# One ring of eight PSUM banks for all stages of a macaron block, in place of one pool per stage

## The chip, the cores and the metric

The kernel runs on one core of one Trainium2 chip. The metric is the device time of one execution in microseconds; the time of the kernel before is the median of three runs, 1818.98 us (1816.17 to 1822.03).

## The reference

Sequence 1024, width 1024, one layer, everything in fp32. The layer is two gated feed-forward blocks with a mixer between them:

```python
h = x
h = h + 0.5 * swiglu_ffn(rmsnorm(h, ffn1_norm), ffn1_w_in, ffn1_w_out)      # d_ff = 2816
u = rmsnorm(h, mix_norm) @ w_mix_in                                         # 1024 x 3592
cb, cc, ch, gq, gk, gv, gz, gb, ga = split(u)
y_conv = rmsnorm_groups(cb * causal_conv3(cc * ch))                         # 512 channels
q, k, v = silu(causal_conv4([gq, gk, gv]))                                  # 4 heads of 128
y_gdn = rmsnorm(gated_delta_rule(l2norm(q), l2norm(k), v, g, beta)) * silu(gz)
h = h + concat([y_conv, y_gdn]) @ w_mix_out
h = h + 0.5 * swiglu_ffn(rmsnorm(h, ffn2_norm), ffn2_w_in, ffn2_w_out)
return rmsnorm(h, final_norm)
```

The gated delta rule is computed by chunks of the sequence: per chunk a masked, decayed product of the keys (`lower`), a triangular system with it, and a step of a state of 128 x 128 per head that goes from chunk to chunk. The kernel uses eight chunks of 128 positions.

## The kernel before

Each large fp32 product is made from three matmuls: an operand is split into a part `hi` and a rest `lo` (ScalarE makes `hi`, VectorE the difference), and `mm3` issues hi by hi, lo by hi and hi by lo, each 128 x 128 by 512 columns, into one PSUM bank (L197, L198, L199). The two feed-forward blocks and the q, k, v projection multiply 2 x 2 blocks by a scheme with seven products in place of eight; the sums of blocks that it needs are made on VectorE and GpSimd and partly kept in HBM.

There are three stages, each inside its own `with ExitStack()`, and each opens its own SBUF pool and its own PSUM pool through `scoped`:

- `f1`: the first feed-forward block (`ffn_in`, `ffn_out`), then the q, k, v projection and the gates (`project_ba`, `finish_ba`). All its banks come from one ring of eight, tag `ps`.
- `mx`: the mixer. Its pool has two rings: four banks `mm` and four banks `aux`. In `mm` lie the projections for z and the short convolution (`unit_steps`: one bank for 8 `mm3`, 24 matmuls), the small reductions of `conv_norm`, the output projection (`mix_out`: one bank for 4 `mm3`), and the column factors of the first half's norm (`norms2[0] = Norm(h2[0], "mm")`, `spread` at L269, read by eight VectorE instructions L305). In `aux` lie the products and transposes of the delta rule: seven tiles per chunk in `build` (decays L1117 and L1120, flips L1060, products L1054), five in `finish` (the blocks of the triangular inverse, L1080, L1261, L1269), five in `scan` (L1054, L1311, and one flip).
- `f2`: the second feed-forward block, again one ring of eight `ps`. The norm of the second half of its input (`norms2[1]`) is reduced and spread in this stage's first steps.

`mx` and `f2` begin with a VectorE memset of one column of their pool's first bank (L1015 and L1613).

The order of work in `mx` is written by hand as Python generators. `build(c)` for eight chunks runs in a pipeline with lag 3; at each step `pump` issues 2.2 `mm3` of the projections, and a step of `late_convs` (four-tap convolutions of v, k, q: ScalarE L953, three VectorE L955, ScalarE L957, store) is taken. Then comes one inversion of all 32 x 32 diagonal blocks on VectorE (`solve`), then `finish` and `scan` for eight chunks in a pipeline with lag 6, beside the remaining projections and `mix_out`. What is traced in this order is then ordered per engine by the framework's planner, ahead of time: it takes, on each engine, the earliest traced instruction that it reckons to be ready, and a tile is given a buffer of its ring only when it reckons one to be free. `tc.keep_in_program_order` holds an instruction behind all that was traced ahead of it on its engine; the reductions and the spreads of norms, the loads of weights (`load`) and the ScalarE part of each split carry it. On the chip each engine then follows its list, and waits by semaphores. A pool whose memory is that of an earlier pool can be used when the earlier pool's tiles have been released.

Of the kernel before, what the change touches and what calls it, by code (L numbers as in the profile page):

```python
# [7 lines left out]
F32 = mybir.dt.float32  # L8
# [4 lines left out]
P = 128  # L13
# [45 lines left out]
def tile_hybrid(  # L59
# [18 lines left out]
    nc = tc.nc  # L78
    PS = bass.MemoryType.PSUM
# [31 lines left out]
    def pool_tt(out, in0, in1, op):  # L111
        tc.keep_in_program_order(nc.gpsimd.tensor_tensor(out=out, in0=in0, in1=in1, op=op))  # L112
# [11 lines left out]
    def run_tasks(to=None, between=None):  # L124
        to = len(tasks) if to is None else to
        while done_to[2] < to:
            stage = 2
            if done_to[1] < min(done_to[2] + AHEAD_PREP + 1, len(tasks)):
                stage = 0 if done_to[0] < min(done_to[1] + AHEAD_LOAD - AHEAD_PREP + 1, len(tasks)) else 1
            f = tasks[done_to[stage]][stage]  # L130
            done_to[stage] += 1
            if f is not None:
                f()
            if stage < 2:
                continue
            if between is not None:
                between()


    scope = {}  # L140

    def psum(tag="ps"):
        bufs = {"ps": 8, "mm": 4, "aux": 4}[tag]
        return scope["ps"].tile([P, 512], F32, name=f"ps_{tag}", tag=tag, bufs=bufs)

    def temp4(dt, name):
        return scope["temp"](dt, name)
# [1 line left out]
    def temp(dt, name):  # L149
        return temp4(dt, name)[:, 3:HALF + 3]  # L150
# [20 lines left out]
    def vcol(i):  # L171
        return vs[:, i:i + 1]
# [16 lines left out]
    def tick():  # L189
        count[0] += 1  # L190
        due = [f for n, f in queue if n <= count[0]]
        queue[:] = [e for e in queue if e[0] > count[0]]
        for f in due:
            f()
# [14 lines left out]
    class Norm:  # L209
# [17 lines left out]
        def reduce(self):  # L227
            cp = psum(self.bank)
            for b in range(4):
                tc.keep_in_program_order(  # L230
                    nc.tensor.matmul(out=cp[:, b:b + 1], lhsT=self.acc[:, b * P:(b + 1) * P], rhs=ones[:, 0:1],
                                     start=True, stop=True))
            self.factor(cp[:, 0:4])
# [9 lines left out]
        def all_landed(self):  # L243
            cp = psum(self.bank)
            for b in range(4):
                tc.keep_in_program_order(
                    nc.tensor.matmul(out=cp[:, b:b + 1], lhsT=self.acc[:, b * P:(b + 1) * P], rhs=one,
                                     start=True, stop=True))
            self.factor(cp[:, 0:4])
# [14 lines left out]
        def spread(self, pinned=True):  # L264

            self.rb = psum(self.bank)
            for b in range(4):
                tc.keep_in_program_order(
                    nc.tensor.transpose(out=self.rb[:, b * P:(b + 1) * P],  # L269
                                        in_=self.rs[:, b:b + 1].broadcast_to([P, P]), identity=ident))  # L270
            for f in self.waiting:
                f()
# [18 lines left out]
    class Blocks:  # L291
# [8 lines left out]
        def gain(self, d):  # L300
            return vcol(self.g + d)
# [398 lines left out]

    def scoped(stack, name, temps=0):
        scope["sb"] = stack.enter_context(tc.tile_pool(name=name, bufs=1))
        scope["ps"] = stack.enter_context(tc.tile_pool(name=name + "ps", bufs=1, space=PS))
        scope["temp"] = lambda dt, n: scope["sb"].tile([P, HALF + 4], dt, name=n, tag="t", bufs=temps)

    def residual(src):

        tiles = [[None] * KT for _ in range(NH)]

        def fill(hf, d):  # L710
            tiles[hf][d] = slot(F32, "h")
            nc.sync.dma_start(out=tiles[hf][d], in_=src[hf][d])

        return tiles, fill
# [4 lines left out]
    h_dr = [[dram.tile([P, HALF], F32, name=f"h_dr{hf}{d}") for d in range(KT)] for hf in range(NH)]  # L719
    with ExitStack() as stack:  # L720
        scoped(stack, "f1", TEMPS)
        x = Blocks(h, "ffn1")
        norms = [Norm(h[hf]) for hf in range(NH)]
# [288 lines left out]

    with ExitStack() as stack:
        scoped(stack, "mx")
        nc.vector.memset(psum("mm")[:, 0:1], 0.0)  # L1015
        mx = scope["sb"]

        def halo(dt, name):
# [591 lines left out]

    with ExitStack() as stack:
        scoped(stack, "f2", TEMPS)
        nc.vector.memset(psum()[:, 0:1], 0.0)  # L1613
        acc, fill = residual(h2_dr)
        last = [Norm(acc[hf]) for hf in range(NH)]

        def pre_scaled(d):
            return d % 3 == 1

        def gain(hf, d):  # L1620
            a = acc[hf][d]
            nc.scalar.activation(out=a, in_=a, func=AF.Copy, scale=vcol(V_N["final"] + d))

        def scale_out(hf, cut=slice(0, HALF)):
            rb = temp(F32, "rbs")
            nc.scalar.copy(out=rb[:, cut], in_=last[hf].rb[:, cut])
            for d in range(KT):
                a = acc[hf][d][:, cut]
                if pre_scaled(d):
                    nc.gpsimd.tensor_tensor(out=a, in0=a, in1=rb[:, cut], op=ALU.mult)  # L1630
                else:
                    nc.vector.scalar_tensor_tensor(out=a, in0=a, scalar=vcol(V_N["final"] + d),
                                                   in1=last[hf].rb[:, cut], op0=ALU.mult, op1=ALU.mult)
                nc.sync.dma_start(out=out[hf, d][:, cut], in_=a)

        def out_t1():
            for d in range(KT):
                last[0].square(d)
            last[0].after(14, 4)
            last[0].then(lambda: [gain(0, d) for d in range(KT) if pre_scaled(d)] and scale_out(0))  # L1640

        def out_t2(d):
            if d == KH - 1:
                last[1].held = temp(F32, "sq")
                nc.scalar.activation(out=last[1].held, in_=acc[1][d], func=AF.Square)
            else:
                last[1].square(d, nc.vector)
            if pre_scaled(d):
                gain(1, d)

        ffn_out(acc, fill, g_dr, w2_out, out_t1, out_t2, by_tile=True)
        run_tasks()

        sums = [psum() for _ in range(2)]
        rbs = [psum() for _ in range(2)]
        ends = [temp(F32, "rbs") for _ in range(2)]
        for n, src in enumerate((last[1].acc, last[1].held)):
            for b in range(4):
                nc.tensor.matmul(out=sums[b // 2][:, b % 2:b % 2 + 1], lhsT=src[:, b * P:(b + 1) * P],
                                 rhs=ones[:, 0:1], start=(n == 0 and b % 2 == 0), stop=(n == 1),  # L1660
                                 skip_group_check=True)
        for i in range(2):
            ms, rs = (const.tile([P, 2], F32, name=f"{n}{i}") for n in ("last_ms", "last_rs"))
            nc.vector.tensor_scalar(out=ms, in0=sums[i][:, 0:2], scalar1=1.0 / D, scalar2=EPS,
                                    op0=ALU.mult, op1=ALU.add)
            nc.gpsimd.tensor_tensor(out=rs, in0=ms, in1=pneg[:, 0:2], op=ALU.pow)
            for b in range(2):
                nc.tensor.transpose(out=rbs[i][:, b * P:(b + 1) * P], in_=rs[:, b:b + 1].broadcast_to([P, P]),
                                    identity=ident)
            nc.scalar.copy(out=ends[i][:, 0:2 * P], in_=rbs[i][:, 0:2 * P])  # L1670
        for i in range(2):
            two = slice(2 * i * P, (2 * i + 2) * P)
            for d in (0, 1, 2, 3, 4, 5, 6, 7):
                a = acc[1][d][:, two]
                if pre_scaled(d):
                    pool_tt(a, a, ends[i][:, 0:2 * P], ALU.mult)
                else:
                    nc.vector.scalar_tensor_tensor(out=a, in0=a, scalar=vcol(V_N["final"] + d),
                                                   in1=rbs[i][:, 0:2 * P], op0=ALU.mult, op1=ALU.mult)
                if i:  # L1680
                    (nc.scalar if d in (1, 2, 5, 7) else nc.sync).dma_start(out=out[1, d], in_=acc[1][d])
        while queue:
            tick()
# [65 lines left out]
```

## Time and profile before

| what | value |
|---|---|
| median of three runs | 1818.98 us (1816.17 to 1822.03) |
| profiled execution | 1819.9 us, span 1818.2 us |
| granted TensorE clock, mean | 0.996 |
| PE busy | 1786.2 us (98%) |
| PE weight loads busy | 1456.0 us (80%) |
| DVE busy | 1333.0 us (73%) |
| ACT busy | 736.7 us (41%) |
| POOL busy | 540.0 us (30%) |
| HBM | 174 GB/s over the span |

The span runs from the first to the last instruction of the program; some 1.7 us of the execution lie around it. Matmuls overlap in the trace: one of 512 columns takes 0.39 us from start to end, but the next one starts 0.23 us after it, so a busy PE need not be at its peak, while a gap of PE is time in which nothing ran. `mx` goes from about 780 to 1168 us of the span.

### The profile page before, as it was taken

To read this page: it belongs to the slowest core of one execution; us is meant where nothing else is said; L and a number is where in the kernel's file an instruction comes from. 1 tells how busy PE (TensorE), PEld (TensorE's weight loads), DVE (VectorE), ACT (ScalarE), POOL (GpSimd) and SP (SyncE) were. 2 spreads that over 40 slices of the span, in tenths; PEclk is the share of its full clock that TensorE was granted. 3 is DMA by queue.
4 is the path that set the end of the run, shared out by engine and by line. 5 is a ranking of instruction groups with operands and counts; after the bars stand their busy time and mean duration, and the time that the engine had idled before them with its cause. 6 is when DMAs were issued, how large, how long until landed. Compare 5 with 4: busy or idle time off the path is not lost.

```text
span 1818.2 us, 24794 instructions
## 1 busy us (share of the span) xinstructions
PE 1786.2 (98%) x8476; PEld 1456.0 (80%) x8476; DVE 1333.0 (73%) x2090; ACT 736.7 (41%) x1471; POOL 540.0 (30%) x382
## 2 busy tenths in 40 slices
PE   9999999999999999999999999999999999999997
PEld 6887788888888877777888877788888888888886
DVE  7898877678776889889575556797666666677675
ACT  7532322223534554468424433552222232344443
POOL 0000034446331412302211102016445554435252
PEclk9999999999999999999999999999999999999998
DMA  7445544336984543478753675523433444487642
GB/s 277 163 129 174 179 146 134 127 116 217 329 270 133 163 156 100 150 239 275 240 186 101 215 255 179 165 73 128 159 125 116 144 140 133 165 304 272 203 143 89
DMA packets 198255, 318.74 MB, mean 175 GB/s; under 512 B 28528, under 2 KB 49008, under 8 KB 198128
## 3 DMA queue, kind: packets, MB, share of 16 engines
q1 hardware_dynamic: 195104, 311.85, 52.0%
q10 hardware_dynamic: 3024, 5.30, 0.8%
q8 instruction: 67, 1.10, 0.3%
q14 instruction: 60, 0.49, 0.1%
HBM read 230.54 MB, written 86.53 MB: 174 GB/s over the span
## 4 chain that ended last, share of the span: by engine, by line
PE 86%; DVE 4%; DMA 4%; ACT 3%; issue 1%; SPq 1%; POOL 1%; POOLq 0%; ACTq 0%; DVEq 0%
PE ps_ps L197 24%; PE ps_ps L199 24%; PE ps_ps L198 24%; PE ps_mm L197 3%; PE ps_mm L198 3%; PE ps_mm L199 3%; DMA raw<-w_in 2%; PE ps_aux L1054 1%; DVE wlo L105 1%; DMA qkv_dr<-cv 1%; PE ps_aux L1060 1%; DVE T L117 1%; DMA gd<-qkv_dr 1%; DVE cv L955 1%; PE ps_aux L1080 0%
## 5 line engine op out<-in xcount | busy, mean ns | idle before, releaser
L197 PE MATMUL ps_ps<-hi,whi 128*128 128x512 f32 x1400 | 547.8, 392 | 5.4 <-DVE c L467 2.8
L199 PE MATMUL ps_ps<-hi,wlo 128*128 128x512 f32 x1400 | 544.7, 390 | 1.0 <-DVE wlo L105 1.0
L198 PE MATMUL ps_ps<-lo,whi 128*128 128x512 f32 x1400 | 545.2, 389 | 0.1
L197 PEld LDWEIGHTS ps_ps<-hi,whi 128*128 128x128 f32 x1400 | 262.8, 188 | 67.7 <-DVE c L467 6.2
L199 PEld LDWEIGHTS ps_ps<-hi,wlo 128*128 128x128 f32 x1400 | 262.8, 188 | 59.2 <-DVE wlo L105 4.5
L198 PEld LDWEIGHTS ps_ps<-lo,whi 128*128 128x128 f32 x1400 | 262.8, 188 | 54.8 <-DVE lo L733 0.6
L112 POOL TENSOR_TENSOR T<-raw 128x512 f32<-128x512 f32 x112 | 173.1, 1546 | 447.2 <-DMA raw<-w_in 225.4
L105 DVE TENSOR_TENSOR wlo<-raw,whi 128x512 fp32r<-128x512 f32 x280 | 238.7, 862 | 71.0 <-ACT whi L104 69.6
L105 DVE TENSOR_TENSOR wlo<-T,whi 128x512 fp32r<-128x512 f32 x244 | 212.6, 883 | 87.2 <-ACT whi L104 85.6
L199 PE MATMUL ps_ps<-ghi,wlo 128*128 128x512 f32 x616 | 241.2, 392 | 0.8 <-DVE wlo L105 0.8
L197 PE MATMUL ps_ps<-ghi,whi 128*128 128x512 f32 x616 | 241.2, 391 | 0.0
L198 PE MATMUL ps_ps<-glo,whi 128*128 128x512 f32 x616 | 240.6, 391 | 0.0
L104 ACT CAST whi<-T 128x512 fp32r<-128x512 f32 x244 | 146.5, 616 | 125.2 <-PE ps_ps L198 41.8
L104 ACT CAST whi<-raw 128x512 fp32r<-128x512 f32 x280 | 168.7, 617 | 58.6 <-PE ps_ps L198 14.6
L105 DVE TENSOR_TENSOR glo<-raw,ghi 128x512 fp32r<-128x512 f32 x154 | 127.7, 829 | 47.2 <-ACT ghi L104 46.6
L197 PE MATMUL ps_mm<-hi,whi 128*128 128x512 f32 x384 | 157.8, 411 | 2.2 <-DVE u L478 1.2
L198 PE MATMUL ps_mm<-lo,whi 128*128 128x512 f32 x384 | 151.9, 396 | 0.0
L199 PE MATMUL ps_mm<-hi,wlo 128*128 128x512 f32 x384 | 151.7, 395 | 0.0
L199 PEld LDWEIGHTS ps_ps<-ghi,wlo 128*128 128x128 f32 x616 | 115.8, 188 | 27.4 <-DVE wlo L105 2.0
L198 PEld LDWEIGHTS ps_ps<-glo,whi 128*128 128x128 f32 x616 | 115.9, 188 | 25.6
L197 PEld LDWEIGHTS ps_ps<-ghi,whi 128*128 128x128 f32 x616 | 115.8, 188 | 25.2
L104 ACT CAST ghi<-raw 128x512 fp32r<-128x512 f32 x154 | 95.0, 617 | 71.1 <-DMA raw<-f1A 19.0
(256 smaller groups left out, 2116.9 us busy)
## 6 DMA issues: line engine op xcount, KB each, us to landing
raw<-w_in SPq DMA_DIRECT2D x264, 256.0 KB, 4.3
raw<-w_out SPq DMA_DIRECT2D x154, 256.0 KB, 4.2
raw<-w_qkv SPq DMA_DIRECT2D x36, 256.0 KB, 3.4
f1S<-S SPq DMA_DIRECT2D x33, 256.0 KB, 4.1
raw<-f1A SPq DMA_DIRECT2D x33, 256.0 KB, 3.8
raw<-f1S SPq DMA_DIRECT2D x33, 256.0 KB, 3.5
f2S<-S SPq DMA_DIRECT2D x33, 256.0 KB, 4.8
raw<-f2A SPq DMA_DIRECT2D x33, 256.0 KB, 4.4
```

What stands on the lines that cost most here:

```text
L104: tc.keep_in_program_order(nc.scalar.copy(out=hi, in_=src))
L105: nc.vector.tensor_tensor(out=lo, in0=src, in1=hi.bitcast(F32), op=ALU.subtract)
L112: tc.keep_in_program_order(nc.gpsimd.tensor_tensor(out=out, in0=in0, in1=in1, op=op))
L117: nc.vector.tensor_tensor(out=out, in0=in0, in1=in1, op=op)
L197: nc.tensor.matmul(out=ps, lhsT=whi, rhs=xhi, start=start, stop=False, skip_group_check=True)
L198: nc.tensor.matmul(out=ps, lhsT=whi, rhs=xlo, start=False, stop=False, skip_group_check=True)
L199: nc.tensor.matmul(out=ps, lhsT=wlo, rhs=xhi, start=False, stop=stop, skip_group_check=True)
L955: nc.vector.scalar_tensor_tensor(out=acc, in0=u[:, i:i + HALF], scalar=vcol(wc + i), in1=acc, op0=ALU.mult, op1=ALU.add)
L1054: nc.tensor.matmul(out=ps[:, sl], lhsT=lhs[:, sl], rhs=rhs[:, sl], start=start, stop=stop)
L1060: nc.tensor.transpose(out=ps[:, sl], in_=src[:, sl], identity=ident)
```

## The change

The PSUM pools of the stages are replaced by one pool `banks`, opened once, with one ring of eight banks under one tag. The argument of `psum` no longer chooses a ring; it only enters the tile's name. `scoped` opens no PSUM pool any more, and the two memsets at the start of `mx` and `f2` are gone. All calls of `psum("mm")`, `psum("aux")` and `psum()` stay as they are, and so does the order in which work is traced. The SBUF pools are not touched.

```diff
+    banks = ctx.enter_context(tc.tile_pool(name="banks", bufs=1, space=PS))
+
-    def psum(tag="ps"):
-        bufs = {"ps": 8, "mm": 4, "aux": 4}[tag]
-        return scope["ps"].tile([P, 512], F32, name=f"ps_{tag}", tag=tag, bufs=bufs)
+    def psum(name="ps"):
+        return banks.tile([P, 512], F32, name=f"ps_{name}", tag="ps", bufs=8)
...
     def scoped(stack, name, temps=0):
         scope["sb"] = stack.enter_context(tc.tile_pool(name=name, bufs=1))
-        scope["ps"] = stack.enter_context(tc.tile_pool(name=name + "ps", bufs=1, space=PS))
...
         scoped(stack, "mx")
-        nc.vector.memset(psum("mm")[:, 0:1], 0.0)
...
         scoped(stack, "f2", TEMPS)
-        nc.vector.memset(psum()[:, 0:1], 0.0)
```

## The prediction

> **What bounds the kernel now.** I read the page's first part, then the list of PE's waits, the table of stretches, and the order of instructions around each wait that the change can touch.
>
> ```profile
> span 1818.2 us, 24794 instructions
> PE 1786.2 (98%) x8476; PEld 1456.0 (80%) x8476; DVE 1333.0 (73%) x2090; ACT 736.7 (41%) x1471; POOL 540.0 (30%) x382
> ```
>
> PE is busy for 1786.2 of 1818.2 us. The change removes no matmul, so it can win at most the 32.0 us in which PE stands still, and anything it costs must appear as new idle time of PE. The profiled execution took 1819.9 us, 1.7 us outside its span and 0.9 us above the median of the runs, 1818.98. I make the sum as a difference and give it for both.
>
> The longest waits of PE, and the shorter ones that concern banks, are these (microseconds in all, times, longest):
>
> ```profile
> PE ps_ps L197 <- DVE c L467: 2.8, 4, 1.6
> PE ps_ps L269 <- POOL rs L225: 1.8, 2, 1.2
> ...
> PE ps_aux L1060 <- DMA gd<-qkv_dr: 1.7, 3, 0.8
> PE ps_aux L1261 <- DVE x L1253: 1.7, 1, 1.7
> PE ps_ps L197 <- DVE h L1562: 1.5, 1, 1.5
> ...
> PE ps_mm L197 <- DVE u L478: 1.2, 1, 1.2
> PE ps_aux L1117 <- DVE r L1110: 1.1, 1, 1.1
> PE ps_aux L1054 <- DVE gd L1286: 1.1, 1, 1.1
> PE ps_mm L197 <- DVE h L305: 1.0, 1, 1.0
> PE ps_aux L1060 <- ACT gd L1333: 1.0, 1, 1.0
> ...
> PE ps_aux L1054 <- ACT junk L1146: 0.4, 1, 0.4
> ```
>
> Which of them are waits for a bank is seen from the code. The matmul of L197 into the first `mm` tile reads nothing that L478 makes; L478 is the last reader of an `f1` bank, so PE waits for the old pool to be given up. In the same way L1562 is the last reader of an `mx` bank ahead of `f2`. L305 reads the spread factors, a bank of the `mm` ring, and the matmuls of `mix_out` behind it read nothing of its result. L1146 reads a flip in `aux` that L1054 doesn't need. That makes four bank waits, 1.2 + 1.5 + 1.0 + 0.4 = 4.1 us. All the others are waits for data: L1253, L1286, L1110 and L1333 make what the waiting matmul reads, and no number of banks shortens them.
>
> Two stretches of the mixer, its build and its scans (columns: length, busy time and count of PE, PEld, DVE, ACT and POOL, granted clock, DMA share, GB/s):
>
> ```profile
> 800.00:860.00 60.00, 57.23 (x302) 46.18 (x303) 55.80 (x123) 52.88 (x128) 11.78 (x8) 1.00 0.86 274
> ...
> 1060.00:1130.00 70.00, 65.97 (x457) 53.28 (x453) 42.75 (x84) 27.79 (x77) 13.43 (x12) 0.98 0.65 205
> ```
>
> In the first, DVE (55.80 of 60) and ACT (52.88) are as full as PE (57.23): there a bank that comes free sooner still waits for its reader. In the second no engine but PE is near full, and PE loses 70.00 - 65.97 = 4.0 us to chains of dependent steps.
>
> **The change part by part.** *From `f1` to `mx`.*
>
> ```profile
> 779.75 0.39 PE L198 MATMUL ps_ps<-lo,whi 128*128 128x512 f32 x1
> 779.98 0.39 PE L199 MATMUL ps_ps<-hi,wlo 128*128 128x512 f32 x1
> 781.55 0.47 PE L197 MATMUL ps_mm<-hi,whi 128*128 128x512 f32 x1 [1.18 <-DVE u L478]
> ...
> 782.07 0.06 DVE L1015 MEMSET ps_mm<- 128x1 f32 x1
> ...
> 798.86 0.39 PE L198 MATMUL ps_mm<-lo,whi 128*128 128x512 f32 x1
> 800.36 0.50 PE L1117 MATMUL ps_aux<-r,mask 128*128 128x512 f32 x1 [1.11 <-DVE r L1110]
> ```
>
> The two PE starts are 1.57 us apart, where the first two rows show matmuls of this kind 0.23 us apart, so the pool's hand-over costs 1.34 us. With one ring the first `mm` tile takes any bank already evacuated. Does the gain survive the next wait, at 800.36 us, where PE stands until DVE has made r0? The rows show PE leaving a triple unfinished (L198 at 798.86, its L199 not yet issued) for L1117: the planner puts in `mm3` work until it reckons r0 ready. If PE comes free 1.34 us sooner in its reckoning too, it fits in some 1.34 / 0.23 = 6 more matmuls ahead of L1117, and these are then missing from later work. I take -1.3; the ends are 0 (L1117 keeps its place behind the same matmuls, and the wait of 1.11 grows) and -1.3.
>
> *The first half's norm in `mx`.*
>
> ```profile
> 1130.98 5.35 DVE L305 SCALAR_TENSOR_TENSOR h<-h,vs,ps_mm 128x512 f32<-128x512 f32 x8
> ...
> 1135.07 0.39 PE L199 MATMUL ps_mm<-hi,wlo 128*128 128x512 f32 x1
> ...
> 1136.47 0.47 PE L197 MATMUL ps_mm<-hi,whi 128*128 128x512 f32 x1 [1.02 <-DVE h L305]
> ```
>
> The spread bank is held until the eight L305 end at 1136.33, and with four banks `mix_out` comes round to it: 1.40 - 0.23 = 1.17 us lost. By then the scans are through, so all eight banks serve `mix_out`, and one held bank leaves seven. A bank there lasts 12 matmuls, 2.7 us, so three more banks reach past the 5.35 us of L305, even though the evacuations L1562 queue behind L305 on DVE. Taken: -1.2, between 0 and -1.2.
>
> *From `mx` to `f2`.*
>
> ```profile
> 1167.37 0.68 DVE L1562 TENSOR_TENSOR h<-ps_mm,h 128x512 f32<-128x512 f32 x1
> 1168.19 0.47 PE L197 MATMUL ps_ps<-hi,whi 128*128 128x512 f32 x1 [1.52 <-DVE h L1562]
> ...
> 1174.57 0.69 DVE L117 TENSOR_TENSOR T<-raw 128x512 f32<-128x512 f32 x1 [2.75 <-DMA raw<-w_in]
> ...
> 1176.50 0.15 DVE L223 TENSOR_SCALAR ms<-ps_ps 128x4 f32<-128x4 f32 x1
> ...
> 1176.74 1.39 POOL L225 TENSOR_TENSOR rs<-ms,cs 128x4 f32<-128x4 f32 x1 [49.51 <-DVE ms L223]
> 1178.17 0.65 PE L269 MATMUL ps_ps<-cs,rs 128*128 128x128 f32 x4 [0.60 <-POOL rs L225]
> ```
>
> The hand-over costs 1.52 us here. But ten microseconds later PE meets L269, the spread of the second half's norm. It is pinned behind 12 `mm3` of `f2` and waits 0.60 us already. Its operand comes over a path on which PE's early start does nothing: the last evacuation at 1167.37, then DVE's queue, in which L223 stands behind two L117 that wait for a weight load until 1174.57, then POOL until 1178.13. If PE starts 1.5 us sooner, it reaches L269 1.5 us sooner and waits 2.1 in place of 0.60. So I take 0, between 0 and -1.5 (the planner may hoist later `mm3` ahead of the spread, or L223 ahead of L117). What is late next here is L223 behind the load of L117, not a bank.
>
> *The memsets.* Each is 0.06 us on DVE, beside PE work: 0, at most -0.1. No DMA and no ACT or POOL instruction is added, removed or moved in the traced order.
>
> *`aux` and `mm` out of one ring.* In `build` a chunk takes seven banks in eight steps, and 2.2 `mm3` go with each step, so a bank of a projection (8 `mm3`) lasts 3.6 steps, in which about 3.2 `aux` banks are handed out. Of eight banks in use about six are then `aux` (four before) and two `mm`. Six ease the `aux` waits: of the 0.4 us behind L1146 I take -0.3, since ACT, which must read the bank, is nearly full in that stretch (between 0 and -0.4). Two `mm` banks mean that a bank is wanted again one unit later, 24 matmuls or 5.5 us, while a reader like L1562 takes 0.68 us. I cost that at 0. The cover is the slack of ACT and DVE; if a reader were held up behind convolution work by more than 5.5 us, PE would stand for the excess.
>
> *The planner's new order.* PE's list is planned under the assumption of which banks are free, so beyond the places above the order of `aux` steps against `mm3` may shift anywhere between 780 and 1168 us. No row shows what that is worth. Bounds come from the stretch 1060 to 1130, where four data waits stand: 1.7 (L1261), 1.1 (L1286), 1.0 (L1333), and, about 1.2, a slow patch behind the first:
>
> ```profile
> 1086.99 0.68 PE L1261 MATMUL ps_aux<-x,gd 64*64 64x64 f32 x8 [1.67 <-DVE x L1253]
> ...
> 1088.26 0.63 PE L197 MATMUL ps_mm<-hi,whi 128*128 128x512 f32 x1
> ...
> 1090.82 0.91 PE L1060 MATMUL ps_aux<-cs,gd 128*128 128x128 f32 x4
> ```
>
> (six matmuls in 2.56 us where 6 x 0.23 = 1.38 is usual). Together they are 5.0 us; a new order may remove them or add as much. I take 0 between -5.0 and +5.0, since nothing in the rows favours a side.
>
> Sum: -1.3 - 1.2 + 0 + 0 - 0.3 + 0 = -2.8 us. That is 1819.9 - 2.8 = 1817.1 for a profiled execution and 1819.0 - 2.8 = 1816.2 for the median.
>
> [...]
>
> **The rivals.** *Given back.* L1117 keeps its place, and the 1.3 us turn into a longer wait for r0; what `mix_out` wins at 1136 is lost to the same pinned L269, whose operand doesn't come sooner. For it speaks that three of the four places are followed by a data wait; against it, the unfinished triple at 798.86, and that the path to L269 starts from an evacuation for which PE's last matmuls are needed, so it moves with PE. Time: 1819, no change.
>
> *Slower: waits in the scans.* With more banks to hand out, the planner places `aux` steps of `finish` and `scan` directly behind one another, where the four-bank ring had forced `mm3` work between them; PE then stands for each DVE step of the chain. Place: 970 to 1130 us. Price per wait: 1.4 us, the mean of 1.7 (L1261) and 1.1 (L1286). It decides from six new waits, 8.4 - 2.8 = +5.6; with one for each of the eight chunks 11.2 - 2.8 = +8.4, 1827. For it: L1261 and L1286 show that the reckoning is already too early on such steps. Against it: only two are late of eighty steps (five banks in `finish` and five in `scan` for eight chunks), and other `mm3` work is at hand.
>
> *Faster: the mixer's waits go.* The bank waits go without being given back, -1.3 - 1.2 - 1.5 - 0.4 = -4.4, and the new order also removes the waits of the scans, -5.0: together -9.4, 1809.6. Half of the second part is enough for -6.9, 1812. For it: PE has filler work at each of these places. Against it: they are waits for data.
>
> *Clock.* Each of the five other waits of about 1 us or more in the mixer (1.5, 1.2, 1.1, 1.1, 1.0) draws a slow patch of 1.2 us: +6.0 - 2.8 = +3.2, 1822. Against it: these same waits drew none before. [...]
>
> **How the numbers follow.** Forecast 0.45, given back 0.15, slower 0.17, faster 0.20, clock 0.03. A measurement of this kernel can tell about 0.3%, 5.5 us. Forecast, given back and clock lie within it: 0.63, less 0.02 each way for the forecast's own tails, which end at -6 and +6. So faster 0.22, same 0.59, slower 0.19. The range goes from 1809 (faster, whole) to 1825 (the planner's +5.0 on top of no gain, and the lower part of the slower rival); by itself the forecast spans 1813 to 1821.
>
> **What would show it.** Right: the first `mm` matmul starts 0.2 us after the last of `f1`; no wait of `mix_out` for L305; the wait of L269 for L225 in `f2` grows from 0.60 to about 2 us; the wait for r0 stays near 1.1. Wrong: new waits of PE on L1253, L1286, L1264 or L1291 in 970 to 1130 us, a granted clock under 1.00 in more stretches, or an `mm` matmul that waits for L1407, L1396 or L1427, the readers of a projection's bank.

## The result, and the profile after

| | before | after |
|---|---|---|
| median of four runs | 1818.92 us (1816.17 to 1822.03) | 1847.24 us (1846.11 to 1848.47) |
| profiled execution, span | 1819.9, 1818.2 us | 1848.0, 1846.3 us |

The change makes the kernel slower: ratio 1.0155, 95% interval 1.0137 to 1.0174, some 28 us, where 2.8 us less were forecast.

The page of after, and PE's waits in it (microseconds in all, times, longest; lines in `mx` have moved up by one):

```profile
span 1846.3 us, 24804 instructions
...
PE 1791.5 (97%) x8476; PEld 1466.7 (79%) x8476; DVE 1338.1 (72%) x2088; ACT 736.8 (40%) x1469; POOL 539.5 (29%) x382
```

```profile
PE ps_aux L1116 <- DVE r L1109: 13.0, 1, 13.0
PE ps_aux L1079 <- DMA xc<-diag_x: 11.0, 1, 11.0
PE ps_aux L1260 <- DVE x L1252: 5.8, 3, 4.3
PE ps_aux L1053 <- DVE gd L1285: 2.7, 3, 1.7
PE ps_ps L198 <- DVE c L468: 1.7, 3, 0.7
```

The waits on L478 and L1562 (the pools) and on L305 (the spread bank) are gone, as the change promised. Two single waits of 13.0 and 11.0 us are new. The three stages of both kernels, before first (length, busy time and count of PE, PEld, DVE, ACT, POOL, granted clock, DMA share, GB/s):

```profile
0.00:781.50 781.50, 772.01 (x3368) 621.60 (x3368) 615.64 (x906) 316.08 (x570) 205.39 (x154) 1.00 0.52 174
781.50:1168.20 386.70, 376.54 (x2293) 309.37 (x2293) 271.11 (x613) 186.19 (x485) 55.15 (x40) 1.00 0.65 208
1168.20:1818.20 650.00, 637.69 (x2816) 525.05 (x2816) 446.25 (x573) 234.42 (x418) 279.51 (x188) 0.99 0.47 158
```

```profile
0.00:777.90 777.90, 770.62 (x3369) 622.67 (x3370) 613.41 (x904) 316.39 (x569) 204.56 (x154) 1.00 0.53 175
777.90:1196.50 418.60, 383.32 (x2294) 319.05 (x2293) 272.45 (x611) 183.94 (x480) 56.56 (x40) 0.95 0.59 192
1196.50:1846.30 649.80, 637.56 (x2817) 524.99 (x2815) 452.20 (x574) 236.49 (x421) 278.40 (x188) 0.99 0.47 158
```

All of the loss lies in the mixer: 386.7 to 418.6 us, +31.9. PE's idle time there grew from 386.70 - 376.54 = 10.2 to 35.3 us, +25.1; the same matmuls were busy 6.8 us longer, at a mean clock of 0.95 in place of 1.00. The first stage is 3.6 us shorter, of which the hand-over is 1.3. PE's list is the same in both kernels up to the mixer's first `aux` tile, so the other 2.3 us are not of the new plan's making; the four runs of the kernel before differ by 5.9 us among themselves.

What stands ahead of the two long waits (PE's instructions in order of time, after):

```profile
777.66 0.39 PE L200 MATMUL ps_ps<-hi,wlo 128*128 128x512 f32 x1
777.88 0.39 PE L198 MATMUL ps_mm<-hi,whi 128*128 128x512 f32 x1
...
783.10 0.39 PE L200 MATMUL ps_mm<-hi,wlo 128*128 128x512 f32 x1
796.50 1.40 PE L1116 MATMUL ps_aux<-r,mask 128*128 128x512 f32 x2 [13.01 <-DVE r L1109]
...
963.27 0.39 PE L200 MATMUL ps_mm<-hi,wlo 128*128 128x512 f32 x1
974.68 0.84 PE L1079 MATMUL ps_aux<-xc,gd 32*32 32x32 f32 x16 [11.02 <-DMA xc<-diag_x]
```

The hand-over is free, 0.22 us from L200 to the first `mm` matmul. Then PE does 24 matmuls, one projection bank, and stands until r0 is there at 796.5. Before, r0 was no earlier (the wait ended at 800.36), but PE had done this meanwhile:

```profile
781.50:799.00 17.50, 17.45 (x77) 14.37 (x77) 12.05 (x19) 10.49 (x19) 0.00 (x0) 1.00 0.82 250
```

77 matmuls of projections in 17.5 us. After had what it needed for the same, as VectorE's rows show:

```profile
778.40 0.68 DVE L479 TENSOR_TENSOR u<-ps_ps,u 128x512 f32<-128x512 f32 x1
...
781.43 2.50 DVE L105 TENSOR_TENSOR lo<-h,hi 128x512 fp32r<-128x512 f32 x4 [0.26 <-ACT hi L104]
```

The last bank of `f1` was read by 779.08 us, so seven of the eight banks were free behind the first projection, and the splits that the second one reads were made by 783.93 us or earlier. The instruction lists that the planner made show why after has only 24. Tiles are numbered in the order in which they are traced; these are the first matmuls into new banks, by row of PE's list (neighbouring instructions on the same tiles count as one row):

```
before                                    after
3342 L197 MATMUL ps_mm_7558               3342 L198 MATMUL ps_mm_7552
3366 L197 MATMUL ps_mm_7653               3366 L1116 MATMUL ps_aux_7561   (r0)
3390 L197 MATMUL ps_mm_7735               3368 L1119 MATMUL ps_aux_7564
3414 L197 MATMUL ps_mm_7825               3370 L1059 MATMUL ps_aux_7584
3419 L1117 MATMUL ps_aux_7567  (r0)       3371 L1059 MATMUL ps_aux_7610
3420 L1120 MATMUL ps_aux_7570             3372 L198 MATMUL ps_mm_7647
```

Within a ring the first uses come in traced order without one exception, in both kernels. Between the two rings of before they don't: `mm` 7653, 7735 and 7825 are used ahead of `aux` 7567. The second wait has the same picture: the first matmul of L1080 (`aux` 9371, traced earlier than `mm` 9431, 9444, 9496 and 9526) stands at row 4047 in before, behind these four, and at row 3998 in after (`aux` 9365 there), ahead of their four counterparts. Theory A is therefore that a ring gives its banks out in traced order: with one ring, a projection traced behind a delta-rule step that waits for data can't begin, though banks are free and its operands are ready. Its rivals: B, the one pool over all stages, without hand-overs and memsets, changed the plan; C, the projections get too few banks once the delta rule takes most of a ring of eight.

### The profile page after: what moved, and what is told of

Same layout as the page of the kernel before. It is cut to its first block, busy times and chain, and to the rows that moved or that the text cites. A ratio compares the mean times of both kernels' runs of the same rounds, so it can differ in the third digit from the quotient of the medians.

```text
span 1846.3 us, 24804 instructions
## 1 busy us (share of the span) xinstructions
PE 1791.5 (97%) x8476; PEld 1466.7 (79%) x8476; DVE 1338.1 (72%) x2088; ACT 736.8 (40%) x1469; POOL 539.5 (29%) x382
## 4 chain that ended last, share of the span: by engine, by line
PE 85%; DVE 6%; DMA 4%; ACT 2%; issue 1%; POOL 1%; SPq 0%; POOLq 0%; ACTq 0%; DVEq 0%
PE ps_ps L198 23%; PE ps_ps L200 23%; PE ps_ps L199 23%; PE ps_mm L198 4%; PE ps_mm L199 4%; PE ps_mm L200 4%; DMA raw<-w_in 2%; PE ps_aux L1053 2%; DVE wlo L105 1%; PE ps_aux L1059 1%; DVE xb L1214 1%; ACT whi L104 1%; DVE sv L1210 1%; DVE T L117 1%; PE ps_aux L1079 0%
## 5 line engine op out<-in xcount | busy, mean ns | idle before, releaser
L200 PE MATMUL ps_ps<-hi,wlo 128*128 128x512 f32 x1400 | 544.4, 390 | 1.3 <-DVE wlo L105 1.3
L200 PEld LDWEIGHTS ps_ps<-hi,wlo 128*128 128x128 f32 x1400 | 262.8, 188 | 58.7 <-DVE wlo L105 3.6
L200 PE MATMUL ps_ps<-ghi,wlo 128*128 128x512 f32 x616 | 241.1, 391 | 0.4 <-DVE wlo L105 0.4
L198 PE MATMUL ps_mm<-hi,whi 128*128 128x512 f32 x384 | 162.6, 423 | 0.0
L105 DVE TENSOR_TENSOR glo<-raw,ghi 128x512 fp32r<-128x512 f32 x154 | 122.8, 797 | 43.0 <-ACT ghi L104 42.2
L200 PE MATMUL ps_mm<-hi,wlo 128*128 128x512 f32 x384 | 152.7, 398 | 0.0
L200 PEld LDWEIGHTS ps_ps<-ghi,wlo 128*128 128x128 f32 x616 | 115.8, 188 | 26.8 <-DVE wlo L105 1.3
```

What stands on the lines that cost most here:

```text
L105: nc.vector.tensor_tensor(out=lo, in0=src, in1=hi.bitcast(F32), op=ALU.subtract)
L198: nc.tensor.matmul(out=ps, lhsT=whi, rhs=xhi, start=start, stop=False, skip_group_check=True)
L200: nc.tensor.matmul(out=ps, lhsT=wlo, rhs=xhi, start=False, stop=stop, skip_group_check=True)
```

## The experiments

**One ring in the mixer, nothing else.** Pools per stage and both memsets are kept.

```diff
-        bufs = {"ps": 8, "mm": 4, "aux": 4}[tag]
-        return scope["ps"].tile([P, 512], F32, name=f"ps_{tag}", tag=tag, bufs=bufs)
+        return scope["ps"].tile([P, 512], F32, name=f"ps_{tag}", tag="ps", bufs=8)
```

> Theories for the 28 us that the change costs. A: a ring gives its banks in the traced order of its tiles, so in one ring no projection can overtake a delta-rule step that waits for data, and PE stands. B: opening one pool over all stages (no hand-over, no memset) changed the plan. C: the projections get too few banks once the delta rule takes most of a ring of eight. This kernel keeps a pool per stage and both memsets, and only merges the mixer's two rings into one of eight. A: as slow as the changed kernel or 1 to 3 us slower, 1847 to 1851, with PE waits of about 13 us on r (first build) and 11 us on diag_x (first finish). B: 1819, neither wait over 2 us. C: 1847 as in A.

1849.56 us (1846.63 to 1851.88), ratio 1.017 (1.0154 to 1.0187). PE's waits:

```profile
PE ps_aux L1116 <- DVE r L1109: 12.6, 1, 12.6
PE ps_aux L1079 <- DMA xc<-diag_x: 10.9, 1, 10.9
...
PE ps_ps L196 <- DVE h L1561: 1.5, 1, 1.5
...
PE ps_mm L196 <- DVE u L477: 1.2, 1, 1.2
```

Both long waits are there, with the hand-overs (1.5 and 1.2) on top. The merged ring alone costs as much as the whole change, 30.8 us in this set of runs; B falls.

**One pool for all stages, two rings.**

```diff
+    turn = [0]
     def psum(name="ps"):
-        return banks.tile([P, 512], F32, name=f"ps_{name}", tag="ps", bufs=8)
+        if name == "ps":
+            turn[0] += 1
+        ring = {"mm": "mm", "aux": "aux", "ps": ("mm", "aux")[turn[0] % 2]}[name]
+        return banks.tile([P, 512], F32, name=f"ps_{name}", tag=ring, bufs=4)
```

> One pool over all stages without memsets, as in the changed kernel, but with two rings of four: mm and aux keep their own, and the tiles of the feed-forward stages take turns between the two. A: neither long wait, PE's gap between the stages gone (first mm matmul 0.2 us behind the last of the first stage), 1814 to 1819. B: as slow as the changed kernel, 1843 to 1849. C: as A.

1814.22 us (1810.38 to 1817.93), ratio 0.9975 (0.9965 to 0.9986): faster than before by some 4.5 us, without either long wait. The r0 step stands at row 3425 of PE's list, six behind before's 3419.

**Fewer banks, rings apart.** The kernel before with `"mm": 2, "aux": 4`; two of eight banks lie idle.

> The kernel before with only two banks in the ring mm, four in aux; two banks of eight are never used. A: the rings are still apart, so neither long wait appears; the held spread bank of the first half's norm costs mix_out some 3 to 5 us more, 1819 to 1826. C: two banks are what the projections had in the shared ring, so the waits of 13 and 11 us or stalls of that size appear, 1840 or more. B: 1819 to 1826.

1828.74 us (1827.24 to 1831.89), ratio 1.0059 (1.0043 to 1.0075). PE's waits:

```profile
PE ps_mm L197 <- DVE h L305: 5.5, 1, 5.5
...
PE ps_aux L1261 <- DVE x L1253: 2.7, 1, 2.7
PE ps_aux L1117 <- DVE r L1110: 2.5, 1, 2.5
```

No wait of 13 or 11 us: with fewer banks than the shared ring, but apart, the projections overtake r0 as before (row 3419). C falls. The time is some 3 us over my upper end: the spread bank, now one of two, costs 5.5 us, and waits that were there grow by 1 to 1.5 us.

**One ring, the fill traced earlier.** The changed kernel, banks as they are:

```diff
-PACE = (2.2, 2.6, 1.5, 1.65)
+PACE = (1.83, 3.5, 1.5, 1.65)
...
-            for _ in main:
-                pump(n_main)
+            for i, _ in enumerate(main):
+                pump(n_main + 24 * (i == 0))
```

> The changed kernel with the traced order altered at the two places: 24 mm3 more are traced behind the first step of the first build (the later steps get 1.83 in place of 2.2, so that the sum stays), and 3.5 in place of 2.6 per pair of solve steps. The banks are as in the changed kernel. A: work that is traced earlier gets its bank earlier, so both long waits fall under 3 us and the clock stays at 1.00 there: 1819 to 1827. B and C: nothing about pools or the number of banks is changed, so 1843 to 1849.

1832.92 us (1831.11 to 1835.26), ratio 1.0081 (1.0065 to 1.0096). PE's waits:

```profile
PE ps_aux L1059 <- ACT gd L1332: 9.2, 2, 5.0
PE ps_aux L1053 <- DVE gd L1285: 5.4, 2, 4.8
...
PE ps_aux L1116 <- DVE r L1109: 0.8, 1, 0.8
```

Both long waits vanish through trace order alone, as A says and neither B nor C does. But 14 of the 28 us remain: in the scans PE now waits for delta-rule steps. I put that down to the projections that were spent early and are missing there; a run below tests it. The time is 6 us over my range.

**The first fill alone** (`PACE[1]` left at 2.6):

> Only the first of the two alterations of the traced order: 24 mm3 more behind the first step of the first build, the later steps 1.83. Theory A (banks are granted in the traced order): the wait on r falls from 13.0 to under 3 us and its slow clock goes, while the wait of 11 us on diag_x and the slow clock behind it stay; 1833 to 1842 (the changed kernel less 13 us and less 3 us of clock, plus what later steps lack in projections). If the two waits have a cause in common other than the order: both go or none.

1837.34 us (1836.28 to 1838.44), ratio 1.0108 (1.009 to 1.0125). The wait on r is 1.1 us, the one on `diag_x` 11.8: the two are separate events, and filling the first gives back 9.9 us of the 28. Filling the second as well (the run ahead of this one) takes away the 11.8 us and gives back only 4.4 us, 1837.34 to 1832.92, as the wait on L1332, in the scans, grows from 1.0 to 9.2 us.

**Where the filled kernel's rest goes.** The same fill in the kernel before (two rings), and the filled one-ring kernel with `PACE = (1.83, 3.5, 1.1, 1.3)`:

> The kernel before, two rings and a pool per stage, with the same two alterations of the traced order as in the run e4 (24 mm3 more behind the first step of the first build, 1.83 for the later ones, 3.5 per pair of solve steps). Question: are the 14 us that e4 still loses against the kernel before due to the altered order or to the one ring? If the order (projections spent early are missing beside the scans): this kernel is as slow as e4, 1829 to 1836. If the one ring: the two rings make good what the order takes, 1817 to 1823, with no wait of PE over 3 us in the scans.

> As the run e4 (one ring, both long waits filled by traced order), with fewer projections and mix_out products per step of the scans: 1.1 in place of 1.5 and 1.3 in place of 1.65, so that filler lasts longer beside the last chunks. If e4's waits of 9.2 us (L1332) and 5.4 us (L1285) come from filler that ran out: they fall under 4 us together and the time goes to 1822 to 1829. If they come from the one ring's order, which holds a pending projection behind an earlier traced delta-rule step: no change or slower, 1830 to 1842.

The kernel before with the fill: 1823.68 us (1819.26 to 1824.51), ratio 1.0026 (1.0014 to 1.0037). One ring with fill and slower pace: 1821.72 us (1817.81 to 1828.12), ratio 1.0021 (1.0007 to 1.0034). So with the altered order the kernel of two rings is some 5 us above the kernel before, the one of one ring 14. The kernel of two rings is 0.7 us over my range for it; its longest wait in the mixer is this:

```profile
PE ps_mm L197 <- ACT hi L104: 3.3, 1, 3.3
```

It is a split for the output projection, not a delta-rule step. With a slower pace one ring too comes to some 0.2% above the kernel before. Of the two waits this is left:

```profile
PE ps_aux L1059 <- ACT gd L1332: 4.9, 2, 4.3
...
PE ps_aux L1053 <- DVE gd L1285: 0.2, 1, 0.2
```

I had put both under 4 us together and the time at 1822 to 1829; the direction holds, the time is 0.3 us below, and L1332 alone is over 4 us. The filler that ran out is thus most of what the filled one-ring kernel lost, 11.2 of its 14 us. No run has the slower pace with two rings, so what one ring costs at that pace isn't known.

**Matmuls without use in the two long waits.** The changed kernel with 56 and 46 matmuls of a zero tile traced ahead of the two steps:

```diff
+            if c == 0:
+                keep_busy(56)
             pd = psum("aux")
...
+            if c == 0:
+                keep_busy(46)
             pl = psum("aux")
```

> The changed kernel with matmuls of a zero tile (bf16, 512 columns, result unused) put into the two long waits: 56 ahead of the first decay product, 46 ahead of the first block product of the inverse. PE has nothing useful to do there in either kernel. Theory A with a clock term: the time of the waits stays, but the granted clock is 1.00 behind them, where the changed kernel has 13.7 and 23.9 us at half; work at half speed behind the waits cost about 2.8 and 7.5 us, so 1834 to 1841. If the clock behind the waits costs nothing (other engines bound there): 1845 to 1850.

Two runs took 1838.5 and 1839.4 us at a mean clock of 0.996, two 1849.6 and 1851.7 us at 0.992 and 0.991; ratio of the medians 1.014 (1.0104 to 1.0175). In the profiled one, 1849.6 us, the clock stays at 1.00 around the first wait (770 to 800 us) but falls behind the second:

```profile
974.00:977.00 3.00, 1.44 (x21) 0.92 (x20) 0.42 (x2) 0.71 (x3) 0.00 (x0) 1.00 0.45 117
977.00:992.00 15.00, 15.00 (x77) 11.74 (x77) 5.53 (x14) 6.28 (x19) 1.63 (x1) 0.55 0.15 43
```

One program thus takes 11.7 us more (the means of the two pairs) where its clock is lower. The ten runs with the slower pace go the same way, from 1817.8 us at 0.994 to 1828.1 at 0.989. That fits a slow patch that costs time, but doesn't show it: no run changed the clock and kept all else. That the patch at 977 us comes from the idle time ahead of it isn't shown either: it came although PE had been kept busy but for 1.6 us. Four runs are few, and the median of 1844.5 lies in neither of my ranges, so this run doesn't decide what the clock is worth.

**The version that wins.** Two rings, and the first half's norm in `aux`, where the scans are nearly over: `Norm(h2[0], "aux")` in place of `"mm"`.

> One pool, two rings of four as in the run e2, and the reduction and spread of the first half's norm moved from the ring mm to aux, where the scans are nearly over. The wait of mix_out for L305 (1.0 us) goes: e2's time less 1 us, 1812 to 1815. If the waiting aux steps of the last scans then hold the reduction up, or its bank holds them up: 1815 to 1820.

1812.78 us (1810.35 to 1817.56), ratio 0.997 (0.9958 to 0.9981). The wait on L305 is gone. It beats both kernels; against the version with the norm in `mm` the intervals overlap.

## Why the prediction was wrong

*From `f1` to `mx`.* The hand-over went as written, 1.57 us between starts to 0.22. The next step failed, that the planner would fit in some six more matmuls ahead of L1117. The new list has 53 rows fewer there. With two rings in one pool it has the six more: the reckoning was right for separate rings.

*`aux` and `mm` out of one ring.* This is the step that failed. I counted how many banks each kind would hold and costed the merging at 0, with the slack of ACT and DVE as its cover. What it cost shows where nothing but the rings is merged: 1849.56 us against 1818.74 of the kernel before, with waits of 12.6 and 10.9 us. The cover was another one: the freedom of projections to run ahead of a delta-rule step. I read the sign of it, the unfinished triple at 798.86, as proof that the planner fills any wait. It can fill only from a ring whose next tile in traced order is ready. The price stood in the trace: 77 matmuls, 17.5 us, between the first `mm` matmul and L1117, while 2.2 `mm3` per step are traced there.

*The planner's new order.* "Between -5.0 and +5.0", from the waits that the trace shows. Such rows bound the waits that are left over; they can't bound a wait that other work hides. The two that came to light are 13.0 and 11.0 us.

*The first half's norm.* Right in its mechanism: no wait on L305 in after. Moving its bank elsewhere (the last run above) does the same without the merged ring.

*From `mx` to `f2`.* I took 0, and expected L269 to wait about 2 us. It doesn't wait (after):

```profile
1202.90 0.16 DVE L224 TENSOR_SCALAR ms<-ps_ps 128x4 f32<-128x4 f32 x1 [0.56 <-PE ps_ps L232]
...
1203.14 1.01 POOL L226 TENSOR_TENSOR rs<-ms,cs 128x4 f32<-128x4 f32 x1 [44.50 <-DVE ms L224]
...
1204.92 0.69 DVE L117 TENSOR_TENSOR T<-raw 128x512 f32<-128x512 f32 x1 [0.97 <-DMA raw<-w_in]
1205.59 0.60 PE L270 MATMUL ps_ps<-cs,rs 128*128 128x128 f32 x4
```

In the new plan the scale step (L224, L223 before) stands ahead of L117 on DVE, not behind it, and the hand-over's 1.5 us are kept. That was the end of the bounds that I had not taken.

*The small `aux` waits.* The one behind L1146 is gone; nothing measurable hangs on it.

*The rivals.* "Slower" had the sign and a part of the place: the waits on L1253 and L1286 grew (5.8 and 2.7 us in after). Why these two grew no run tells. They are the smaller part: the two long waits make 24.0 us, where PE's idle time in the mixer grew by 25.1 in all, and their cause is the order of grants, not `aux` steps that follow one another because more banks are free. "Clock" had a part of the size: behind both long waits the clock is at half (after):

```profile
796.50:800.50 4.00, 4.00 (x13) 3.30 (x14) 4.00 (x7) 2.62 (x4) 0.00 (x0) 0.50 0.94 268
...
974.70:990.00 15.30, 14.93 (x90) 12.42 (x91) 3.82 (x12) 5.19 (x18) 1.64 (x1) 0.51 0.21 56
```

Of the mixer's +31.9 us, 6.8 are longer busy time. The condition that I gave, many waits of about 1 us, wasn't it.

*The span of the forecast.* That "by itself the forecast spans 1813 to 1821" doesn't follow from my terms, since 1816.2 - 5.0 is 1811. The measured time lies far outside either.

What stays open: how the second wait and the waits of the scans add up was tested only through fills; no run removed the second wait without the first.

## What to carry to other kernels

A ring of buffers is also a queue: where tiles are granted in traced order, two kinds of work that share a ring can't overtake each other, whatever number of buffers is free. Keep work that fills waits in another ring than the work that waits, and share the pool, not the ring, to save the hand-over between stages. When an edit could take away a cover, price it from the work that now runs beside the late operand (here 17.5 us), not from the small waits that are left.

## What the runs showed of the hardware

The low clock lasted longer than in the mixer of the kernel before, where it stood at 0.50 in one patch, from 1088.1 to 1091.4 us, 3.3 us. In after it was at 0.50 around the two long waits, from 788.3 to 802.0 us and from 965.9 to 989.8 us. Behind the second wait it stayed at 0.51 with PE busy 14.93 of 15.30 us, as the profile counts it, and in the kernel with matmuls of zeros it was at 0.55 over 15 us of busy PE. In the stretch of 15.30 us in after, 56 of the 90 matmuls are of 32 x 32 (40) and 64 x 64 (16). In the kernel before, from 969 to 990 us, 128 of 216 were such (96 and 32), among projections and without a wait ahead of them, and the clock was 1.00:

```profile
969.00:990.00 21.00, 21.00 (x216) 16.39 (x215) 12.40 (x33) 13.03 (x41) 1.01 (x1) 1.00 0.38 109
```

Why the clock stayed low for 15 us of busy PE in the one and not in the other, no run tells.
